# mLSTM numerators: 128-row products first, 64-row ones in pairs of row halves; mask, LN(v) and head-norm passes on ScalarE

## The chip, the cores and the metric

The kernel runs on one core of a Trainium2 chip. The metric is the device time of one execution in microseconds (us), and the median of several executions is quoted. The engines are named as the profile names them: PE is TensorE's matmuls, PEld its weight loads, DVE is VectorE, ACT is ScalarE, POOL is GpSimd and SP is the queue that issues the DMAs.

## The reference

One layer of a hybrid network works on 1024 latent tokens and 256 context tokens of width 1024. Here only the part that the change touches is written out; `h` is a normalised and modulated input.

```python
u, v, q, k, vv, o, gates = split(h @ W_in)
yA = u * (W_s @ LN(v; g_v, b_v) + b_s)      # per chunk of 128 tokens, 4 groups of 128 channels
# mLSTM, 4 heads, forward and backward, chunks of 128 tokens (rows t, sources s):
dmat    = where(tri, b_t - b_s + i_s, -inf)
w_intra = exp(dmat - m_t);   w_inter = exp(b_t + m0 - m_t)
scores  = (q k^T) * w_intra
num     = scores @ vv + w_inter * (q @ C0)  # C0: 64 x 128 state of the chunk's start
den     = sum(scores) + w_inter * (q @ n0)
h_head  = num / max(|den|, exp(-m_t))
yB      = sigmoid(o) * HeadNorm(h_fwd + h_bwd)
x = LN1(ALPHA * x + gate1 * ([yA | yB] @ W_out))
x = LN2(ALPHA * x + gate2 * SqReLU_MLP(...))
```

A head has 64 key channels and 128 value channels. So `scores @ vv` sums over 128 sources, and `q @ C0` over 64 channels.

## The kernel before

The kernel is one long program, written stage by stage in Python. A tile framework orders it: each engine works through its own list in order, the lists are laid out by the framework's scheduler, and semaphores hold an instruction until its inputs are ready and its output buffer is free. All matrix products of the projections are made of three products of rounded parts (`mm3`, lines 206 to 209: weight or activation, each split into a high and a low part); each is one pass of 512 columns. The small products of the mLSTM take float32 operands as they are, and the trace shows each of them as two passes.

The stage that the change touches (lines 802 to 830) runs from 226 to 364 us of the trace. It goes over eight chunks `j` of 128 tokens:

- `d_load(j)` loads keys `kc`, values with a column of ones `vac`, queries `qd`, and rows spread over partitions: `wib` (w_inter) and `nmb` (minus m). There is one `nmb` buffer for each direction `d`, four in all, two chunks' worth.
- `d_weights(j)` makes the weights exp(dmat - m): for each direction and head a pass on DVE (line 706) adds a column and the triangular mask, then one pass on ACT for four heads (line 707) takes the exponential. It also scales `wib` by the queries (line 708).
- `d_scores(j)` makes q k^T with 64 rows a head (line 716). Heads of even number lie on partitions 0 to 63, those of odd number on 64 to 127, and the two have PSUM banks of their own. DVE then multiplies the weights in (line 720).
- `d_out(j, d, b)` makes numerators and denominators of one direction and two heads in one PSUM bank: for each head a product of 128 rows (line 735, `vac` and the weighted scores) and one of 64 rows (line 736, the state `St` and `wib`). Direction 0 of `wib` and `St` lies on partitions 0 to 63, direction 1 on 64 to 127. Then DVE makes the reciprocal of the denominator (lines 739 to 742), and ACT (line 746) or DVE (line 748) divides.
- `d_norm(j)` normalises a head's 128 channels: statistics on DVE, a power on POOL (line 760), four passes on DVE (line 762), and a DMA to memory.

Between these stand the fillers: eight units `v_unit(j)` (24 passes of 512 columns each, then LN(v) in two DVE passes, lines 669 and 670, and later a small product `mix` with W_s, line 677, and its DVE pass, line 679) and four units `u_unit` of the same size. After each `d_out` and `d_scores` the loop takes one piece of six passes from the fillers. What is left of them runs after the loop, and then the output projection and the MLP, with 760 us to come.

[...] Banks 0 to 2 (`mm`) serve the large products, 3 and 4 (`tr`) transposes and `mix`, 5 to 7 (`nm`) the scores and numerators.

## Time and profile before

| | us |
|---|---|
| median of 3 executions | 1126.34 |
| lowest and highest | 1125.40 and 1127.55 |
| the profiled execution | 1127.33 |
| span of that execution, first to last instruction | 1125.40 |

The profile is of one execution. The span leaves out 1.93 us ahead of the first and behind the last instruction. A matmul's row in the trace is longer than its turn: passes overlap, and what counts is the distance from one start to the next. The rows are read for three things: which engine's chain ends last, how far matmuls of each kind stand apart, and what the other engines have left to do in the same stretch.

### The profile page before, as it was taken

What the parts mean: (1) busy time and instruction counts of PE and PEld (TensorE: products, weight loads), DVE (VectorE), ACT (ScalarE), POOL (GpSimd) and SP (SyncE); (2) the same over time, 40 slices, a digit from 0 to 9 for tenths busy, and PEclk for the clock granted to TensorE, in tenths of its full rate; (3) what the DMA queues carried; (4) which work ended last, traced back from release to release, by engine and by line L of the source; (5) the groups of instructions that cost most, each with busy time, mean ns of one, the idle gap of its engine ahead of it and who ended that gap; (6) DMA issues with size and microseconds to landing.
All of it is one profiled execution on the core that took longest, in us unless ns stands there. A gap on an engine that the chain in (4) does not pass through costs nothing.

```text
span 1125.4 us, 14624 instructions
## 1 busy us (share of the span) xinstructions
PE 1094.6 (97%) x5271; PEld 899.9 (80%) x5271; DVE 761.5 (68%) x1363; ACT 517.6 (46%) x821; POOL 53.6 (5%) x81
## 2 busy tenths in 40 slices
PE   8999999899999999997999999999999999999996
PEld 6899788777777888885888888888888888887875
DVE  4793666677775367659974747474667555468997
ACT  3585543321121236567755555556534334434341
POOL 0010000000101011110000000000000000001101
PEclk9999999999999999998999999999999999999999
DMA  8782579776453773233454435355997334356911
GB/s 319 259 280 95 169 255 293 236 204 175 127 155 113 260 238 129 85 112 112 151 195 127 175 123 183 112 197 201 321 413 271 113 90 152 96 168 235 326 57 75
DMA packets 92416, 208.08 MB, mean 185 GB/s; under 512 B 10037, under 2 KB 31413, under 8 KB 92089
## 3 DMA queue, kind: packets, MB, share of 16 engines
q1 hardware_dynamic: 92344, 207.16, 55.0%
q8 instruction: 41, 0.67, 0.2%
q14 instruction: 31, 0.25, 0.1%
HBM read 155.91 MB, written 51.21 MB: 184 GB/s over the span
## 4 chain that ended last, share of the span: by engine, by line
PE 89%; DVE 4%; DMA 3%; ACT 2%; issue 1%; POOL 1%; SPq 0%; DVEq 0%; ACTq 0%; POOLq 0%
PE A L986 29%; PE B L986 23%; PE wo L209 3%; PE wo L207 3%; PE wo L208 3%; PE n L736 2%; PE n L735 2%; PE pa L270 2%; PE v L207 2%; PE vg L209 1%; PE vg L208 1%; PE vg L207 1%; PE u L207 1%; PE v L209 1%; PE v L208 1%; PE u L209 1%
## 5 line engine op out<-in xcount | busy, mean ns | idle before, releaser
L986 PE MATMUL A<-wh,pb 128*128 128x512 f32 (+1 forms) x528 | 158.6, 383 | 0.0
L986 PE MATMUL B<-wh,pb 128*128 128x512 f32 x384 | 118.7, 390 | 0.0
L986 PEld LDWEIGHTS A<-wh,pb 128*128 128x128 f32 x528 | 98.0, 188 | 19.8
L986 PE MATMUL A<-wl,pb 128*128 128x512 f32 (+1 forms) x264 | 101.7, 385 | 3.2 <-DVE nmu_n L874 1.5
L986 PEld LDWEIGHTS B<-wh,pb 128*128 128x128 f32 x384 | 72.1, 188 | 15.6
L986 PE MATMUL B<-wl,pb 128*128 128x512 f32 x192 | 74.9, 390 | 0.0
L1206 ACT CAST pb<-a_S 128x1024 fp32r<-128x1024 f32 x32 | 33.7, 1053 | 75.1 <-PE B L986 43.8
L880 POOL TENSOR_TENSOR rs_n<-ve_n,mhalf 128x1 f32<-128x1 f32 x23 | 29.4, 1279 | 720.2 <-DVE ve_n L878 681.4
L1113 DVE TENSOR_TENSOR wc<-w1x,wc 128x512 fp32r<-128x512 f32 x56 | 38.3, 692 | 35.9 <-ACT wc L1112 35.9
L1207 DVE TENSOR_TENSOR wl<-b,wh 128x1024 fp32r<-128x1024 f32 x40 | 48.7, 1222 | 19.9 <-ACT wh L1206 6.9
L986 PEld LDWEIGHTS A<-wl,pb 128*128 128x128 f32 x264 | 49.6, 188 | 14.5 <-DVE nmu_n L874 1.7
L1207 DVE TENSOR_TENSOR pb<-a_S,pb 128x1024 fp32r<-128x1024 f32 x32 | 39.1, 1223 | 31.7 <-ACT pb L1206 31.5
L1206 ACT CAST wh<-b 128x1024 fp32r<-128x1024 f32 x40 | 42.0, 1051 | 33.4 <-DVE pb L1207 16.0
L207 PE MATMUL wo<-lo_W,yh 128*128 128x512 f32 x128 | 52.0, 406 | 0.0
L209 PE MATMUL wo<-hi_W,yl 128*128 128x512 f32 x128 | 50.7, 396 | 0.0
L208 PE MATMUL wo<-hi_W,yh 128*128 128x512 f32 x128 | 50.5, 394 | 0.0
L207 PE MATMUL vg<-lo_VG,Hhi 128*128 128x264 f32 x160 | 45.9, 287 | 0.0
L209 PE MATMUL vg<-hi_VG,Hlo 128*128 128x264 f32 x160 | 45.4, 284 | 0.5 <-DVE Hlo L198 0.5
L707 ACT ACTIVATE nmb<-nmb 128x512 f32<-128x512 f32 x16 | 10.1, 633 | 76.8 <-DVE nmb L706 46.6
L208 PE MATMUL vg<-hi_VG,Hhi 128*128 128x264 f32 x160 | 45.3, 284 | 0.0
L1112 ACT CAST wc<-w1x 128x512 fp32r<-128x512 f32 x56 | 34.4, 619 | 22.4 <-PE A L986 10.6
L1206 ACT CAST pb<-a_A 128x1024 fp32r<-128x1024 f32 x24 | 25.3, 1054 | 41.4 <-PE A L986 20.3
(412 smaller groups left out, 2773.7 us busy)
## 6 DMA issues: line engine op xcount, KB each, us to landing
ad<-in_wada SPq DMA_DIRECT2D x32, 512.0 KB, 6.1
b<-in_w SPq DMA_DIRECT2D x32, 512.0 KB, 5.2
a_S<-d_S SPq DMA_DIRECT2D x32, 512.0 KB, 4.1
d_S<-hF SPq DMA_DIRECT2D x50, 256.0 KB, 2.2
a_A<-d_A SPq DMA_DIRECT2D x24, 512.0 KB, 5.0
d_A<-hF SPq DMA_DIRECT2D x36, 256.0 KB, 2.0
wa<-in_wada SPq DMA_DIRECT2D x16, 512.0 KB, 6.2
w1x<-in_w SPq DMA_DIRECT2D x16, 512.0 KB, 3.6
```

What stands on the lines that cost most here:

```text
L207: T.matmul(o, ahi, blo, start=start, stop=False)
L208: T.matmul(o, ahi, bhi, start=False, stop=False)
L209: T.matmul(o, alo, bhi, start=False, stop=stop)
L270: T.matmul(pa[:, 0:256], s32[:, k, :], rv[k // 4][:, k % 4, :], start=(k == 0), stop=(k == KT - 1))
L735: T.matmul(pn[:, hh, :], nmb[d][:, h, :], vc[:, h, :], start=True, stop=False)
L736: T.matmul(pn[:, hh, :], wib[o : o + 64, h, :], st[o : o + 64, h, :], start=False, stop=True)
L880: G.tensor_tensor(rs, ve, mhalf[:, :1], op=ALU.pow)
L986: T.matmul(o, a, b, start=start and i == 0, stop=stop and i == 2, skip_group_check=more)
L1112: S.copy(t[:, 0:512], src)
L1113: V.tensor_tensor(t[:, 512:1024], src, t[:, 0:512].bitcast(F32), ALU.subtract)
L1206: S.copy(hi, src)
L1207: V.tensor_tensor(lo, src, hi.bitcast(F32), ALU.subtract)
```

## The change

It leaves the arithmetic of the layer as it is and changes its order and its engines in the stage described above.

- The numerators of both directions of two heads are made together (`d_out_mm`): four products of 128 rows, then four of 64 rows that alternate between the two halves of the partitions, in two PSUM banks. The loop puts the scores of the next chunk behind the second such group. Division stays as it was but comes as a step of its own (`d_out_ev`).
- The mask is added by one DVE pass for four heads, and the column is the bias of the exponential, which ACT now takes for each head apart: 8 passes a chunk instead of 2. The two directions share one `nmb` tile, with two buffers.
- LN(v): the second DVE pass goes; ACT scales by the reciprocal deviation. The offset `b_v` goes through W_s once, in a product `mix_bias` ahead of the loop, into the offset of the mix.
- The head norm: DVE makes a small product (`hnb`), and ACT makes the four passes.
- The numerators' ring of PSUM banks grows from three banks to five (3 to 7) for this stage, and `mix` moves to the ring of the large products.
- The loop takes two pieces of the fillers at each of three places.

```diff
--- before.py
+++ after.py
@@ -72,8 +72,10 @@
     def ps_tr(name):
         return ps_next("tr", 3, 2, name).rearrange("p (a b) -> p a b", a=4)
 
+    nm_ring = [5, 3]
+
     def ps_nm(name):
-        return ps_next("nm", 5, 3, name)
+        return ps_next("nm", *nm_ring, name)
 
 
     def prep_slot(src, n, name, colscale=None):
@@ -667,12 +669,19 @@
         mv, rs = stats(dp, pm, 512, f"v{j}")
         vc = ka.tile([P, 512], F32, tag="f2k", bufs=4, name=f"vc_{j}")
         V.scalar_tensor_tensor(vc, pm, mv[:, 0:1], lnv[:, 0, :], ALU.subtract, ALU.mult)
-        V.scalar_tensor_tensor(vc, vc, rs, lnv[:, 1, :], ALU.mult, ALU.add)
+        S.activation(vc, vc, AF.Copy, scale=rs)
         vpend.append((j, vc))
         yield
 
+    def mix_bias():
+
+        px = ps_mm("mixb").rearrange("p (a b) -> p a b", a=4)
+        for g in range(4):
+            T.matmul(px[:, g, :], lnv[:, 1, g * P : (g + 1) * P], wsT[:, g, :], start=True, stop=True)
+        V.tensor_tensor(bsb, px, bsb, ALU.add)
+
     def v_unit_mix(j, vc):
-        px = ps_tr(f"mix_{j}")
+        px = ps_mm(f"mix_{j}").rearrange("p (a b) -> p a b", a=4)
         for g in range(4):
             T.matmul(px[:, g, :], vc[:, g * P : (g + 1) * P], wsT[:, g, :], start=True, stop=True)
         mx = ka.tile([P, 4, P], F32, tag="f2k", bufs=4, name=f"mx_{j}")
@@ -686,25 +695,23 @@
         kc, vc = load_kv(j)
         qd = dp.tile([P, NH, P], F32, tag="qd", name=f"qd_{j}")
         wib = dp.tile([P, NH, P], F32, tag="wib", name=f"wib_{j}")
-        nmb = []
+        nmb = dp.tile([P, 2, NH, P], F32, tag="nmb", bufs=2, name=f"nmb_{j}")
         for d in range(2):
             o = 64 * d
             for hh in range(2):
                 dma(qd[o : o + 64, hh : hh + 3 : 2, :], d_q[64 * hh : 64 * hh + 64, :, j * P : (j + 1) * P])
             dma(wib[o : o + 64], d_rows[1, d, j].partition_broadcast(64))
-            t = dp.tile([P, NH, P], F32, tag="nmb", bufs=4, name=f"nmb_{j}_{d}")
-            dma(t, d_rows[0, d, j].partition_broadcast(P))
-            nmb.append(t)
+            dma(nmb[:, d], d_rows[0, d, j].partition_broadcast(P))
         dstate[j] = [kc, vc, qd, wib, nmb]
 
     def d_weights(j):
         kc, vc, qd, wib, nmb = dstate[j][:5]
         for d in range(2):
             r = rowbase[d](j)
-            w = nmb[d]
+            w = nmb[:, d]
+            V.tensor_tensor(w, w, mask[d].unsqueeze(1).broadcast_to([P, NH, P]), ALU.add)
             for h in range(NH):
-                V.scalar_tensor_tensor(w[:, h, :], w[:, h, :], a_cols[:, r + h : r + h + 1], mask[d], ALU.add, ALU.add)
-            S.activation(w, w, AF.Exp)
+                S.activation(w[:, h, :], w[:, h, :], AF.Exp, bias=a_cols[:, r + h : r + h + 1])
         V.scalar_tensor_tensor(wib, qd, QSCALE, wib, ALU.mult, ALU.mult)
 
     def d_scores(j):
@@ -715,37 +722,46 @@
             o = 64 * hh
             T.matmul(pss[hh][:, b * P : (b + 1) * P], kc[o : o + 64, b, :], qd[o : o + 64, h, :], start=True, stop=True)
         for hh in range(2):
+            sc = pss[hh][:, 0:256].rearrange("p (b t) -> p b t", b=2)
             for d in range(2):
-                wv = nmb[d].rearrange("p (b h) t -> p h b t", h=2)
-                V.scalar_tensor_tensor(
-                    wv[:, hh], pss[hh][:, 0:256].rearrange("p (b t) -> p b t", b=2), QSCALE, wv[:, hh], ALU.mult, ALU.mult
+                wv = nmb[:, d].rearrange("p (b h) t -> p h b t", h=2)
+                V.scalar_tensor_tensor(wv[:, hh], sc, QSCALE, wv[:, hh], ALU.mult, ALU.mult)
+
+    def d_out_mm(j, b):
+
+        kc, vc, qd, wib, nmb = dstate[j][:5]
+        pn = [ps_nm(f"n_{j}_{d}_{b}")[:, 0:258].rearrange("p (h v) -> p h v", h=2) for d in range(2)]
+        for d in range(2):
+            for hh in range(2):
+                h = 2 * b + hh
+                T.matmul(pn[d][:, hh, :], nmb[:, d, h, :], vc[:, h, :], start=hh == 0, stop=False, skip_group_check=True)
+        for hh in range(2):
+            for d in range(2):
+                h, o = 2 * b + hh, 64 * d
+                st = St[(step_f, step_b)[d](j)]
+                T.matmul(
+                    pn[d][:, hh, :], wib[o : o + 64, h, :], st[o : o + 64, h, :], start=False, stop=hh == 1, skip_group_check=True
                 )
-
-    def d_out(j, d, b):
-        kc, vc, qd, wib, nmb = dstate[j][:5]
-        if d == 0 and b == 0:
+        return pn
+
+    def d_out_ev(j, b, pn):
+        if b == 0:
             dstate[j].append(dp.tile([P, NH, P], F32, tag="hs", name=f"hs_{j}"))
         hs = dstate[j][5]
-        r = rowbase[d](j)
-        o = 64 * d
-        st = St[(step_f, step_b)[d](j)]
-        pn = ps_nm(f"n_{j}_{d}_{b}")[:, 0:258].rearrange("p (h v) -> p h v", h=2)
-        for hh in range(2):
-            h = 2 * b + hh
-            T.matmul(pn[:, hh, :], nmb[d][:, h, :], vc[:, h, :], start=True, stop=False)
-            T.matmul(pn[:, hh, :], wib[o : o + 64, h, :], st[o : o + 64, h, :], start=False, stop=True)
-        dn = dp.tile([P, 2], F32, tag="dn", bufs=4, name=f"dn_{j}_{d}_{b}")
-        den = pn[:, :, 128:129]
-        V.tensor_tensor(dn.unsqueeze(2), den, em_cols[:, r + 2 * b : r + 2 * b + 2].unsqueeze(2), ALU.max)
-        V.scalar_tensor_tensor(dn.unsqueeze(2), den, -1.0, dn.unsqueeze(2), ALU.mult, ALU.max)
-        rc = dp.tile([P, 2], F32, tag="rc", bufs=4, name=f"rc_{j}_{d}_{b}")
-        V.reciprocal(rc, dn)
-        for hh in range(2):
-            h = 2 * b + hh
-            if d == 0:
-                S.activation(hs[:, h, :], pn[:, hh, 0:P], AF.Copy, scale=rc[:, hh : hh + 1])
-            else:
-                V.scalar_tensor_tensor(hs[:, h, :], pn[:, hh, 0:P], rc[:, hh : hh + 1], hs[:, h, :], ALU.mult, ALU.add)
+        for d in range(2):
+            r = rowbase[d](j)
+            dn = dp.tile([P, 2], F32, tag="dn", bufs=4, name=f"dn_{j}_{d}_{b}")
+            den = pn[d][:, :, 128:129]
+            V.tensor_tensor(dn.unsqueeze(2), den, em_cols[:, r + 2 * b : r + 2 * b + 2].unsqueeze(2), ALU.max)
+            V.scalar_tensor_tensor(dn.unsqueeze(2), den, -1.0, dn.unsqueeze(2), ALU.mult, ALU.max)
+            rc = dp.tile([P, 2], F32, tag="rc", bufs=4, name=f"rc_{j}_{d}_{b}")
+            V.reciprocal(rc, dn)
+            for hh in range(2):
+                h = 2 * b + hh
+                if d == 0:
+                    S.activation(hs[:, h, :], pn[d][:, hh, 0:P], AF.Copy, scale=rc[:, hh : hh + 1])
+                else:
+                    V.scalar_tensor_tensor(hs[:, h, :], pn[d][:, hh, 0:P], rc[:, hh : hh + 1], hs[:, h, :], ALU.mult, ALU.add)
 
     def d_norm(j):
         hs = dstate[j][5]
@@ -758,8 +774,10 @@
         V.tensor_scalar(ve.unsqueeze(2), mv[:, :, 1:2], EPS, None, ALU.add)
         rs = dp.tile([P, NH], F32, tag="hrs", name=f"hrs_{j}")
         G.tensor_tensor(rs, ve, mhalf, op=ALU.pow)
+        nb = dp.tile([P, NH], F32, tag="hnb", name=f"hnb_{j}")
+        V.scalar_tensor_tensor(nb.unsqueeze(2), mv[:, :, 0:1], -1.0, rs.unsqueeze(2), ALU.mult, ALU.mult)
         for h in range(NH):
-            V.tensor_scalar(hs[:, h, :], hs[:, h, :], mv[:, h, 0:1], rs[:, h : h + 1], ALU.subtract, ALU.mult)
+            S.activation(hs[:, h, :], hs[:, h, :], AF.Identity, bias=nb[:, h : h + 1], scale=rs[:, h : h + 1])
         dma(d_z[j], hs.rearrange("p h v -> p (h v)"))
 
     wU = []
@@ -800,31 +818,32 @@
             yield from u_unit(ka, "f2k", 4, blk, 0)
 
     fill = fillers()
+    nm_ring[:] = [3, 5]
+    mix_bias()
     d_load(0)
     d_load(1)
     d_weights(0)
     next(fill)
     next(fill)
     d_scores(0)
-    steps = 0
     for j in range(NT):
-        todo = []
         if j + 1 < NT:
-            todo.append(lambda j=j: d_weights(j + 1))
-        todo.append(lambda j=j: d_out(j, 0, 0))
-        todo.append(lambda j=j: d_out(j, 0, 1))
+            d_weights(j + 1)
+        pn = d_out_mm(j, 0)
+        d_out_ev(j, 0, pn)
+        next(fill, None)
+        next(fill, None)
+        pn = d_out_mm(j, 1)
         if j + 1 < NT:
-            todo.append(lambda j=j: d_scores(j + 1))
-        todo.append(lambda j=j: d_out(j, 1, 0))
-        todo.append(lambda j=j: d_out(j, 1, 1))
+            d_scores(j + 1)
+        d_out_ev(j, 1, pn)
+        next(fill, None)
+        next(fill, None)
         if j + 2 < NT:
-            todo.append(lambda j=j: (d_load(j + 2), d_norm(j)))
-        else:
-            todo.append(lambda j=j: d_norm(j))
-        for i, f in enumerate(todo):
-            f()
-            if i > 0:
-                next(fill, None)
+            d_load(j + 2)
+        d_norm(j)
+        next(fill, None)
+        next(fill, None)
     run(fill)
     dd.close()
     pd.close()
```

On PE, the numerators of chunk 1 in direction 1 and around them, with the scores of chunk 2, stood before like this (`n_d_b` is the bank of direction `d` and heads 2b and 2b+1, `S_0` and `S_1` are the scores of the two halves of the partitions; one row is one float32 product, that is two passes):

```order
L677 MATMUL mix_2768<-wsT,vc_2716 128x128 x4
L716 MATMUL S_0_2776<-qd_2668,kc_2664 128x128 x2
L207 MATMUL v_2743<-lo_V_2289,Hhi 128x512
L208 MATMUL v_2743<-hi_V_2288,Hhi 128x512
L209 MATMUL v_2743<-hi_V_2288,Hlo 128x512
L207 MATMUL v_2743<-lo_V_2289,Hhi 128x512
L716 MATMUL S_1_2777<-qd_2668,kc_2664 128x128 x2
L208 MATMUL v_2743<-hi_V_2288,Hhi 128x512
L209 MATMUL v_2743<-hi_V_2288,Hlo 128x512
L207 MATMUL v_2743<-lo_V_2289,Hhi 128x512
L208 MATMUL v_2743<-hi_V_2288,Hhi 128x512
L735 MATMUL n_1_0_2792<-vac_2496,nmb_1_2508 128x129
```

and the same place reads now:

```order
L686 MATMUL mix_2773<-wsT,vc_2721 128x128 x4
L737 MATMUL n_0_1_2781<-vac_2501,nmb_2505 128x129 x2
L737 MATMUL n_1_1_2782<-vac_2501,nmb_2505 128x129 x2
L742 MATMUL n_0_1_2781<-St_1752,wib_2504 128x129
L742 MATMUL n_1_1_2782<-St_1757,wib_2504 128x129
L742 MATMUL n_0_1_2781<-St_1752,wib_2504 128x129
L742 MATMUL n_1_1_2782<-St_1757,wib_2504 128x129
L723 MATMUL S_0_2791<-qd_2666,kc_2662 128x128
L723 MATMUL S_1_2792<-qd_2666,kc_2662 128x128
L723 MATMUL S_0_2791<-qd_2666,kc_2662 128x128
L723 MATMUL S_1_2792<-qd_2666,kc_2662 128x128
L209 MATMUL v_2760<-lo_V_2289,Hhi 128x512
```

The eight products of 64 rows stand together now and alternate between the halves; before, the scores of one half stood apart from those of the other, with filler passes between. In two of the 16 groups a `mix` or filler passes come between the products of 64 rows, here for chunk 4:

```order
L737 MATMUL n_0_0_3269<-vac_3024,nmb_3028 128x129 x2
L737 MATMUL n_1_0_3270<-vac_3024,nmb_3028 128x129 x2
L742 MATMUL n_0_0_3269<-St_1755,wib_3027 128x129
L686 MATMUL mix_3250<-wsT,vc_3195 128x128 x4
L742 MATMUL n_1_0_3270<-St_1754,wib_3027 128x129
L742 MATMUL n_0_0_3269<-St_1755,wib_3027 128x129
L742 MATMUL n_1_0_3270<-St_1754,wib_3027 128x129
```

There one product of 64 rows is parted from the other three.

On DVE, the mask of chunk 4 and what surrounds it stood before like this (`hve` feeds POOL's power, `st_v`, `mv_v` and `ve_v` are the statistics of LN(v), `vc` its result):

```order
L178 BN_STATS st_v_3066<-v_2971 128x6
L756 BN_AGGR hmv_3038<-hst_3_3048 128x2
L706 SCALAR_TENSOR_TENSOR nmb_0_3031<-nmb_0_3031,cols,cst 128x128
L758 TENSOR_SCALAR hve_3051<-hmv_3038 128x4
L180 BN_AGGR mv_v_3068<-st_v_3066 128x2
L706 SCALAR_TENSOR_TENSOR nmb_0_3031<-nmb_0_3031,cols,cst 128x128
L762 TENSOR_SCALAR hs_2913<-hs_2913,hmv_3038,hrs_3053 128x128 x4
L169 TENSOR_SCALAR ve_v_3070<-mv_v_3068 128x1
L669 SCALAR_TENSOR_TENSOR vc_3074<-v_2971,mv_v_3068,lnv 128x512
L706 SCALAR_TENSOR_TENSOR nmb_0_3031<-nmb_0_3031,cols,cst 128x128
L670 SCALAR_TENSOR_TENSOR vc_3074<-vc_3074,rs_v_3072,lnv 128x512
L706 SCALAR_TENSOR_TENSOR nmb_1_3036<-nmb_1_3036,cols,cst 128x128 x4
```

and now:

```order
L712 TENSOR_TENSOR nmb_3028<-nmb_3028,cst 128x512
L772 BN_AGGR hmv_3037<-hst_3_3047 128x2
L715 SCALAR_TENSOR_TENSOR wib_3027<-qd_3026,wib_3027 128x512
L688 TENSOR_TENSOR mx_3019<-mix_3014,bsb 128x512
L774 TENSOR_SCALAR hve_3050<-hmv_3037 128x4
L712 TENSOR_TENSOR nmb_3028<-nmb_3028,cst 128x512
L778 SCALAR_TENSOR_TENSOR hnb_3054<-hmv_3037,hrs_3052 128x4
L180 BN_STATS st_v_3073<-v_3001 128x6
L182 BN_AGGR mv_v_3075<-st_v_3073 128x2
L171 TENSOR_SCALAR ve_v_3077<-mv_v_3075 128x1
L671 SCALAR_TENSOR_TENSOR vc_3081<-v_3001,mv_v_3075,lnv 128x512
```

Both mask passes stand ahead of the statistics of LN(v) now. On ACT the same chunk reads now (before, two rows of line 707 and nothing else of these):

```order
L714 ACTIVATE nmb_3028<-nmb_3028,cols 128x128 x5
L780 ACTIVATE hs_2929<-hs_2929,hnb_3054,hrs_3052 128x128 x4
L714 ACTIVATE nmb_3028<-nmb_3028,cols 128x128 x3
L672 ACTIVATE vc_3081<-vc_3081,rs_v_3079 128x512
L762 ACTIVATE hs_3105<-n_0_0_3095,rc_0_0_3109 128x128 x2
```

The scaling of `vc`, on which the next `mix` waits, stands behind the exponentials and the head norm. On every engine but SP the instructions behind this stage are the same and in the same order as before; on PE that holds from the last numerator on.

## Rows read from the trace of the kernel before

**Rows 1.** The chain that ended last, by engine, share of the span (page, part 4)

```profile
PE 89%; DVE 4%; DMA 3%; ACT 2%; issue 1%; POOL 1%; SPq 0%; DVEq 0%; ACTq 0%; POOLq 0%
```

**Rows 2.** Busy time by stretches; count, granted clock and DMA share as its header says

```profile
core 0: us, PE busy (x) PEld busy (x) DVE busy (x) ACT busy (x) POOL busy (x), PEclk, DMA share, GB/s
...
226.00:246.00 20.00, 20.00 (x102) 14.57 (x101) 16.29 (x58) 7.01 (x11) 0.55 (x1) 1.00 0.68 194
```

**Rows 3.** All that PE waited for from 226 to 390 us: total, times, longest

```profile
PE mix L677 <- DVE vc L670: 0.3, 1, 0.3
```

**Rows 4.** PE in time: start, length, engine, line, out<-in, rows*columns, count

```profile
229.33 0.39 PE L208 MATMUL v<-hi_V,Hhi 128*128 128x512 f32 x1
229.56 0.39 PE L209 MATMUL v<-hi_V,Hlo 128*128 128x512 f32 x1
229.87 0.71 PE L716 MATMUL S<-qd,kc 64*128 64x128 f32 x8
230.52 0.50 PE L207 MATMUL v<-lo_V,Hhi 128*128 128x512 f32 x1
230.86 0.39 PE L208 MATMUL v<-hi_V,Hhi 128*128 128x512 f32 x1
...
231.32 0.38 PE L735 MATMUL n<-vac,nmb 128*128 128x129 f32 x2
231.64 0.49 PE L736 MATMUL n<-St,wib 64*128 64x129 f32 x2
232.05 0.49 PE L735 MATMUL n<-vac,nmb 128*128 128x129 f32 x2
232.47 0.49 PE L736 MATMUL n<-St,wib 64*128 64x129 f32 x2
232.89 0.50 PE L207 MATMUL v<-lo_V,Hhi 128*128 128x512 f32 x1
```

**Rows 5.** PE in time: scores of one half of the partitions alone

```profile
256.21 0.71 PE L716 MATMUL S<-qd,kc 64*128 64x128 f32 x4
256.85 0.50 PE L208 MATMUL v<-hi_V,Hhi 128*128 128x512 f32 x1
```

**Rows 6.** PE in time: eight passes of 128 rows in a row

```profile
242.02 1.05 PE L677 MATMUL mix<-wsT,vc 128*128 128x128 f32 x8
242.91 0.39 PE L735 MATMUL n<-vac,nmb 128*128 128x129 f32 x2
```

**Rows 7.** Groups by line, 226 to 346 us: count, busy us and mean ns, idle before

```profile
L706 DVE SCALAR_TENSOR_TENSOR nmb<-nmb,cols,cst 128x128 f32<-128x128 f32 x64 | 19.2, 343 | 2.1 <-DMA nmb<-d_rows 2.1
L762 DVE TENSOR_SCALAR hs<-hs,hmv,hrs 128x128 f32<-128x128 f32 x24 | 6.7, 344 | 4.4 <-POOL hrs L760 4.4
L670 DVE SCALAR_TENSOR_TENSOR vc<-vc,rs_v,lnv 128x512 f32<-128x512 f32 x8 | 6.0, 746 | 0.0
L679 DVE TENSOR_TENSOR mx<-mix,bsb 128x512 f32<-128x512 f32 x8 | 5.5, 686 | 4.9 <-PE mix L677 4.9
...
L707 ACT ACTIVATE nmb<-nmb 128x512 f32<-128x512 f32 x16 | 10.1, 633 | 76.8 <-DVE nmb L706 46.6 <-issue 26.6 <-DVE hve L758 3.7
```

**Rows 8.** ACT in time: two passes of 128x128

```profile
233.65 0.63 ACT L746 ACTIVATE hs<-n,rc 128x128 f32<-128x128 f32 x2 [3.08 <-DVE rc L742]
```

**Rows 9.** SP in time, and what nmb's DMAs take from issue to landing

```profile
261.73 0.33 SPq L43 DMA_DIRECT2D vac<-d_va  x1
...
263.34 0.54 SPq L43 DMA_DIRECT2D nmb<-d_rows  x1
...
DMA to landing us min/median/max: 3.4/4.9/6.6
```

**Rows 10.** The one wait of PE, all engines in time

```profile
325.25 0.35 DVE L706 SCALAR_TENSOR_TENSOR nmb<-nmb,cols,cst 128x128 f32<-128x128 f32 x1 [0.66 <-DMA nmb<-d_rows]
...
326.32 0.38 PE L677 MATMUL mix<-wsT,vc 128*128 128x128 f32 x1 [0.33 <-DVE vc L670]
```

**Rows 11.** Weight loads of the mix products, 226 to 346 us

```profile
L677 PEld LDWEIGHTS mix<-wsT,vc 128*128 128x128 f32 x64 | 8.1, 191 | 1.4 <-DVE vc L670 0.8
```

## The prediction

> **What bounds the kernel now.** I read the chain that ended last first: PE has 89% of the span [rows 1]. [...] Then PE's waits: from 226 to 390 us, through the stage and 26 us behind it, PE waited for another engine once, for 0.3 us [rows 3]. So what ends last in this stage is PE's own list. An edit is worth what it takes off that list, and work that moves from DVE to ACT is worth nothing by itself; it matters only if it makes somebody late. Last I read the list's spacing, start to start.
>
> **What PE's passes cost.** A filler pass takes 0.23 us (229.33 to 229.56) [rows 4]. A pass of 128 rows and 128 columns takes 0.111: eight `mix` passes in 0.89 us [rows 6]. Passes of 64 rows cost a toll on both sides. The scores of chunk 0 start 0.31 us behind the last filler pass (0.08 more than it needs), their eight passes take 0.65, and the next filler pass takes 0.34 (0.11 more) [rows 4]: 0.84 for the visit. Scores of one half alone take 0.64 for four passes [rows 5], 0.83 with the same two tolls. So eight passes that alternate between the halves cost no more than four of one half: they run in pairs.
>
> What is toll and what is work follows from one `d_out`: 231.32 to 232.89 is 1.57 us, 1.68 with the 0.11 behind it [rows 4]. It holds four passes of 128 rows (0.44), four of 64 rows in one half, and two visits, since the list goes 735, 736, 735, 736. So 4 passes + 2 tolls = 1.24 and 4 passes + 1 toll = 0.83: the toll is 0.41 us a visit, a pass of 64 rows or a pair of them 0.105.
>
> **The change part by part.**
>
> Numerators. One chunk and pair of heads takes two `d_out` now, 3.36 us. Then it takes eight passes of 128 rows (0.89) and one visit of eight alternating passes (0.84, as the scores of chunk 0), 1.73 us. That is 1.63 less, 16 times: 26.1 us.
>
> Scores. Chunks 0 and 1 cost 0.84 each; the order shows chunks 2 to 7 with two visits each, 1.66 us. Sum 11.6. Then chunk 0 costs 0.84, and seven chunks follow the state products directly, so they pay four pairs (0.42 to 0.43) and no toll: 3.0. That saves 7.8 us.
>
> Taken away from that: `mix_bias` adds eight passes, 0.89 us, on PE's path. Two of the 16 groups are parted in the order, each one more toll of 0.41 and in one an unpaired product of two passes, about 0.2: 1.0 us. PE's list becomes 26.1 + 7.8 - 0.9 - 1.0 = 32.0 us shorter.
>
> DVE. The masks were 64 passes, 19.2 us, and become 16 of 512 columns, by line 679's 0.686 us [rows 7] 11.0. Line 670 goes, 6.0 us, and line 762, 32 passes of 0.344, 11.0 [rows 7]. The small product and `mix_bias`'s pass add at most eight and one passes of that 0.344 and 0.686, 3.4 together. DVE has some 21 us less in a stage that is 32 us shorter, so its share stays about where it is. ACT takes 64 exponentials for 16 of 0.633 us [rows 7]; two passes of 128 columns take 0.63 [rows 8], so 20.2 for 10.1, and 10.1 for the head norm and about 5.1 (eight of 0.633) for LN(v): 25 us more on an engine that was busy 7.01 of 20 us in its fullest window here [rows 2]. None of this lies on PE's path; PE's own list covers it, as long as results come in time.
>
> The wait that it adds. Both directions of `nmb` are one tile now, so its next load waits for all numerators of the chunk. Behind them SP issues `vac`, `wib`, `nmb`, `wib`, `nmb`; from `vac` to the first `nmb` took 1.61 us behind two `wib` [rows 9], so the second stands some 2.2 us behind the last numerator, and lands 3.4 to 6.6 us later, 4.9 in the median [rows 9]: at 7.1, with ends of 5.6 and 8.8. DVE stands at the second mask pass until then, ahead of the statistics of LN(v); ACT has the rest of the exponentials and the head norm ahead of scaling `vc`; and PE needs that `vc` for the next `mix`. This is the kind of wait that PE had once before: DVE stood 0.66 us for `nmb`, and `mix` came 0.33 us late [rows 10]. PE is there after a second's scores and exit (0.6), 12 filler passes (2.76), a `mix` (0.89), 12 passes (2.76), a group (1.73) and 12 passes (2.76): 11.5 us behind the last numerator. With the median landing the mask ends at 7.8; ACT then has one exponential, four norm passes and three exponentials at 0.31 each (2.5) and `vc` (0.63): 10.9 at the earliest, 0.6 before it is needed. With the latest landing 12.6, 1.1 late. Six loads of chunks 2 to 7 make 0 to 6.6 us. I take 2, nearer the median, since not every one is followed by a `mix` at that distance.
>
> **Sum.** 32.0 - 2.0 = 30.0 us. The profiled execution took 1127.33 us with its span of 1125.40, 1 us over the median of 1126.34. So 1097.3 against itself, and 1096.3 against the median; I say 1096.5.
>
> **A rule against it.** The `mix` passes follow each other at 0.111 us though each has a weight load of 0.191 us [rows 6, 11], so loads overlap passes of the same rows. [...] The trace contradicts it for `mix` and I give it 2 in 100.
>
> **Rivals.**
>
> The loads come later than I take them: bunched behind one wait they share the DMA engines with each other and with weights, and DVE and ACT are in order behind them. Waits of 4 to 10 us, time 1098.5 to 1104.5. For it speaks the one wait of before; against it that PE's banks and the next numerators have several us of slack.
>
> The pairs don't form for the state products: unlike the scores these add onto a bank that others have begun. Then four more pass times of 0.105 in each of 16 groups, 6.8 us: 1103. Against it: they lie as the scores lie, halves in turn and a bank for each half.
>
> The change doesn't do what it says: the order decides that, and it shows 14 of 16 groups whole. All 16 broken would cost 0.41 or 0.6 us each, 14 of which aren't in the sum: 6 to 8 us, 1104. It is in the chance of the rival before.
>
> Slower: the `nmb` loads set the pace. Then PE would have to wait more than 5.3 us at each of the six places to lose all 32. Given the 0.6 us of slack behind a median landing, the landing would have to take over 4.9 + 0.6 + 5.3 = 10.8 us from its issue; the longest was 6.6. At 12 us for each the kernel takes 1134.
>
> No change: the gain is given back behind the stage, where the output projection waits for its weights. Against it: PE waited for nothing in the 26 us behind the stage [rows 3], and the buffers for these loads come free as PE gets through the list, which moves as a whole.
>
> **How the numbers follow.** Forecast, waits up to 4 us, 1094 to 1098.5: 0.66. Late loads: 0.18. No pairs or broken ones: 0.09. The rule on weight loads: 0.02. No change: 0.03. Slower: 0.02. The range leaves out the last two and the ends of the others: 1092 (no new wait, and a little less toll than worked out) to 1104. A measurement of this kernel tells about 0.2% from no change: faster 0.95, same 0.03, slower 0.02.
>
> **What would show it.** In the profile after, a group should take about 1.7 us from its first numerator to the next filler pass, state products should start in pairs, and scores should follow them within 0.45 us. PE should still be busy all through the stage, its end some 30 us earlier, with the waits of PE listed at `mix` behind ACT's `vc`. If state products start 0.1 us apart one by one, the pairs failed. If PE's waits sum to over 10 us, DVE or ACT, or `nmb`'s landing, has become the bound, and the forecast is wrong.

## The result, and the profile after

The changed kernel takes 1107.09 us (median; 1106.29 to 1108.06) against 1126.94 before: ratio 0.983, 95% interval 0.981 to 0.984. That is 19.9 us less where 30 were forecast, and 3 us above the range.

The list of PE became what was worked out. In time order, PE in the changed kernel (as [rows 4]): a whole group of numerators, and one with the scores right behind it.

```profile
244.05 1.05 PE L737 MATMUL n<-vac,nmb 128*128 128x129 f32 x8
245.03 0.71 PE L742 MATMUL n<-St,wib 64*128 64x129 f32 x8
245.68 0.50 PE L209 MATMUL v<-lo_V,Hhi 128*128 128x512 f32 x1
246.02 0.40 PE L210 MATMUL v<-hi_V,Hhi 128*128 128x512 f32 x1
...
251.85 0.72 PE L742 MATMUL n<-St,wib 64*128 64x129 f32 x8
252.41 0.61 PE L723 MATMUL S<-qd,kc 64*128 64x128 f32 x8
252.95 0.50 PE L209 MATMUL v<-lo_V,Hhi 128*128 128x512 f32 x1
```

From 244.05 to 245.68 and the 0.11 that the next filler pass takes too long make 1.74 us; the prediction said 1.73. State products with the scores behind them end after 1.10, which is 0.45 more than the 0.65 of state products alone; it said 0.42 to 0.43.

What is new are waits. All that PE waited for from 226 to 390 us, total, times and longest (as [rows 3], which had 0.3 us):

```profile
PE mix L686 <- ACT vc L672: 6.0, 4, 3.0
PE u L209 <- DVE vc L671: 2.3, 1, 2.3
```

The windows (as [rows 2]; in each row PE's busy time is the first number behind the length, and the granted clock stands behind POOL's) show a second loss:

```profile
226.00:246.00 20.00, 20.00 (x130) 16.43 (x130) 15.89 (x51) 9.75 (x28) 0.55 (x1) 1.00 0.78 209
246.00:266.00 20.00, 17.75 (x111) 14.77 (x110) 15.27 (x59) 10.86 (x29) 3.12 (x4) 1.00 0.86 251
286.00:306.00 20.00, 17.02 (x91) 14.19 (x90) 11.02 (x42) 7.45 (x19) 1.76 (x3) 0.83 0.49 115
...
289.00:292.40 3.40, 0.43 (x3) 0.24 (x2) 2.17 (x6) 1.45 (x4) 0.55 (x1) 0.99 0.86 218
292.40:299.20 6.80, 6.79 (x23) 5.56 (x24) 2.62 (x13) 2.34 (x8) 0.00 (x0) 0.50 0.13 42
```

After the longest wait PE worked 6.8 us at a granted clock of 0.50, with filler passes 0.43 us apart (296.17 to 296.60) instead of 0.23, and by that clock lost 3.4 us. So 8.3 us of waits and 3.4 of half clock, 11.7 us, were paid out of the shorter list.

How the longest wait came about, all engines in time order (start, length; in brackets the idle time before and what ended it):

```profile
285.02 0.39 PE L211 MATMUL v<-hi_V,Hlo 128*128 128x512 f32 x1
285.44 0.70 DVE L180 BATCH_NORM_STATS2 st_v<-v 128x6 f32<-128x512 f32 x1
...
288.38 0.69 DVE L712 TENSOR_TENSOR nmb<-nmb,cst 128x512 f32<-128x512 f32 x1 [1.51 <-DMA nmb<-d_rows]
288.95 0.49 PE L742 MATMUL n<-St,wib 64*128 64x129 f32 x2
288.99 0.17 DVE L182 BATCH_NORM_AGGREGATE mv_v<-st_v 128x2 f32<-128x6 f32 x1
...
290.11 0.69 DVE L715 SCALAR_TENSOR_TENSOR wib<-qd,wib 128x512 f32<-128x512 f32 x1 [0.95 <-issue]
290.72 0.14 DVE L171 TENSOR_SCALAR ve_v<-mv_v 128x1 f32<-128x1 f32 x1
290.79 0.74 DVE L671 SCALAR_TENSOR_TENSOR vc<-v,mv_v,lnv 128x512 f32<-128x512 f32 x1
...
291.64 0.72 ACT L672 ACTIVATE vc<-vc,rs_v 128x512 f32<-128x512 f32 x1 [1.78 <-DVE vc L671]
...
292.42 2.08 PE L686 MATMUL mix<-wsT,vc 128*128 128x128 f32 x8 [2.98 <-ACT vc L672]
```

The first statistics pass of LN(v) was done at 286.1. Then DVE stood at a mask for the first `nmb` until 288.38, took the mask, the aggregate, stood at the `wib` product until 290.11, and only then made `vc`. The mask of the second `nmb` came behind that, at 291.44. The profile names no releaser for the last 0.95 us at the `wib` product; the second `wib`, issued at 283.92, landed 5.8 us later. The chain of waits of that stretch, from 280 to 296 us (start, length, what; its first row gives shares by line), names the same load:

```profile
by line: DMA wib<-d_rows 32.7%; PE mix L686 16.5%; PE n L742 11.3%; issue 9.8%; SPq L43 5.8%; PE n L737 5.6%; ACT vc L672 4.6%; PE v L209 4.5%; DVE wib L715 4.3%; DVE vc L671 4.2%; PE S L723 3.1%; DVE ve_v L171 0.4%; ACTq L672 0.2%
...
283.92 5.24 DMA wib<-d_rows
...
290.11 0.69 DVE wib L715
```

Not every wait was one for loads. For the wait of 2.3 us at `u`, DVE had stood only 0.27 us for `nmb`; two passes that round weights for a later stage (line 92) stood ahead of LN(v) there:

```profile
309.06 0.69 DVE L712 TENSOR_TENSOR nmb<-nmb,cst 128x512 f32<-128x512 f32 x1 [0.27 <-DMA nmb<-d_rows]
310.10 2.35 DVE L92 TENSOR_TENSOR lo_W<-raw_W,hi_W 128x1024 fp32r<-128x1024 f32 x2
312.37 0.69 DVE L180 BATCH_NORM_STATS2 st_v<-v 128x6 f32<-128x512 f32 x1
...
314.18 0.50 PE L209 MATMUL u<-Hlo,hi_U 128*128 128x512 f32 x1 [2.28 <-DVE vc L671]
```

For the wait of 0.8 us at 279.3, the first pass of `vc` was done at 277.51, and ACT then finished a norm pass and took three exponentials ahead of the scaling:

```profile
277.66 0.97 ACT L714 ACTIVATE nmb<-nmb,cols 128x128 f32<-128x128 f32 x3
278.54 0.71 ACT L672 ACTIVATE vc<-vc,rs_v 128x512 f32<-128x512 f32 x1
```

For each v unit I read two times from such rows, counted from the end of its last pass: when `vc` is ready, and when PE, waits aside, has come to the `mix` that needs it (for unit 7 of the changed kernel, less the 2.3 us at `u`). Unit 5 above: the last pass ends at 285.41, `vc` is ready at 292.37 (6.96), PE is free at 292.42 - 2.98 = 289.44 (4.03).

| v unit | before: vc ready | before: PE there | after: vc ready | after: PE there |
|---|---|---|---|---|
| 0 | 3.9 | 5.1 | 3.3 | 4.8 |
| 1 | 5.5 | 6.0 | 5.6 | 4.5 |
| 2 | 4.1 | 6.2 | 4.0 | 2.9 |
| 3 | 4.9 | 7.5 | 2.8 | 4.8 |
| 4 | 5.1 | 6.5 | 5.2 | 4.5 |
| 5 | 3.2 | 4.3 | 7.0 | 4.0 |
| 6 | 3.3 | 5.9 | 2.6 | 4.8 |
| 7 | 6.4 | 6.1 | 6.1 | 4.1 |
| mean | 4.55 | 5.94 | 4.57 | 4.29 |

In the mean LN(v) is no later than before. PE is 1.65 us earlier, because the groups that lie between are shorter, and `vc` comes unevenly: 2.6 to 4.0 us where no mask stands ahead, up to 7.0 where DVE waits for loads.

### The profile page after: what moved, and what is told of

It is laid out like the page before. It is cut to its first block, busy times and chain, and to the rows that moved or that the text cites. A ratio compares the mean times of both kernels' runs of the same rounds, so it can differ in the third digit from the quotient of the medians.

```text
span 1103.4 us, 14609 instructions
## 1 busy us (share of the span) xinstructions
PE 1065.2 (97%) x5279; PEld 885.6 (80%) x5279; DVE 743.2 (67%) x1284; ACT 543.9 (49%) x909; POOL 52.8 (5%) x81
## 4 chain that ended last, share of the span: by engine, by line
PE 85%; DVE 5%; DMA 4%; ACT 2%; issue 1%; POOL 1%; SPq 0%; DVEq 0%; ACTq 0%; POOLq 0%
PE A L1005 29%; PE B L1005 23%; PE wo L211 3%; PE wo L209 3%; PE wo L210 3%; PE pa L272 2%; DMA nmb<-d_rows 2%; PE vg L211 2%; PE vg L210 1%; PE vg L209 1%; PE u L209 1%; PE u L210 1%; PE u L211 1%; PE o L211 1%; PE o L209 1%
## 5 line engine op out<-in xcount | busy, mean ns | idle before, releaser
L1226 DVE TENSOR_TENSOR wl<-b,wh 128x1024 fp32r<-128x1024 f32 x40 | 48.7, 1221 | 19.9 <-ACT wh L1225 6.9
L1226 DVE TENSOR_TENSOR pb<-a_A,pb 128x1024 fp32r<-128x1024 f32 x24 | 29.3, 1221 | 21.1 <-ACT pb L1225 21.0
```

The source lines that it names most:

```text
L1226: V.tensor_tensor(lo, src, hi.bitcast(F32), ALU.subtract)
```

## The experiments

All kernels have the changed one as their base, but for one that starts from the kernel before; diffs show what differs. An edit also lets the framework set the order on DVE, ACT and SP anew where times change in its own estimate, so a difference of 2 or 3 us can come from that (e8 gained its 3.3 us that way). PE's order stays nearly the same; the largest difference is e14's, where the scores stand in 11 pieces (8 or 9 in the others with the new order). In the table, waits are PE's from 226 to 390 us; half clock is (1 - granted clock) x 20 us summed over the windows from 226 to 366; the rest is the span less both.

| kernel | median us | ratio to before, 95% | span | waits | half clock | rest |
|---|---|---|---|---|---|---|
| changed | 1107.1 | 0.981-0.984 | 1103.4 | 8.3 | 3.4 | 1091.7 |
| e1 products alone | 1102.2 | 0.977-0.981 | 1100.3 | 4.7 | 1.8 | 1093.8 |
| e2 third nmb | 1101.7 | 0.975-0.981 | 1100.8 | 5.9 | 5.2 | 1089.7 |
| e3 vc on DVE | 1110.8 | 0.985-0.989 | 1109.0 | 11.3 | 7.2 | 1090.5 |
| e4 norm on DVE | 1102.3 | 0.978-0.981 | 1100.7 | 6.6 | 1.8 | 1092.3 |
| e5 mix 0-6 later | 1105.1 | 0.980-0.983 | 1104.0 | 8.7 | 5.2 | 1090.1 |
| e6 other bank | 1105.9 | 0.981-0.984 | 1103.1 | 8.5 | 5.2 | 1089.4 |
| e7 all mix later | 1102.0 | 0.978-0.981 | 1100.5 | 5.3 | 3.4 | 1091.8 |
| e8 moves alone | 1122.1 | 0.996-0.998 | 1118.4 | 0.0 | 0.0 | 1118.4 |
| e9 masks behind LN | 1097.6 | 0.972-0.976 | 1096.0 | 3.8 | 0.0 | 1092.2 |
| e10 and third nmb | 1095.1 | 0.970-0.974 | 1093.9 | 2.6 | 0.0 | 1091.3 |
| e11 and mix later | 1093.1 | 0.969-0.972 | 1092.4 | 0.9 | 0.0 | 1091.5 |
| e12 two nmb tiles | 1100.1 | 0.975-0.979 | 1097.6 | 5.2 | 1.8 | 1090.6 |
| e13 e11 in sequence | 1092.5 | 0.968-0.972 | 1089.7 | 1.1 | 0.0 | 1088.6 |
| e14 e9 without moves | 1101.7 | 0.977-0.980 | 1099.1 | 3.9 | 3.4 | 1091.8 |

The last column is the main finding: in the 14 kernels with the new order of products it is 1091.1 in the mean and within 2.7 of it in each. Before it is 1125.4 - 0.3 = 1125.1, which is 34 us more. The column is what is left of one execution's whole span, so it carries what varies outside of the stage too. Inside the stage, from the first V pass to the first pass behind the last U pass, the kernel before and then the changed one show:

```profile
226.93 0.50 PE L207 MATMUL v<-lo_V,Hhi 128*128 128x512 f32 x1
388.98 0.60 PE L864 MATMUL pzt<-cst,zt 128*128 128x128 f32 x4
```

```profile
227.10 0.47 PE L209 MATMUL v<-lo_V,Hhi 128*128 128x512 f32 x1
367.83 0.60 PE L883 MATMUL pzt<-cst,zt 128*128 128x128 f32 x4
```

That is 162.05 and 140.73 us; without waits and half clock 161.7 and 129.0, so 32.7 less, and 31.8 once the 0.9 of `mix_bias`, which stands ahead of the first V pass, is counted. The same reading of the other kernels with the new order gives 30.1 to 33.2 (32.0 were worked out). So the list became shorter about as forecast in all of them, and they differ mainly by what PE waits and by the half clock behind the waits.

**First: loads, moves to ACT, or DVE's load?** The new order of products with DVE's old work (masks, LN(v), head norm):

```
-            V.tensor_tensor(w, w, mask[d]..., ALU.add)          # and exponentials by head with bias
+            V.scalar_tensor_tensor(w[:, h, :], ..., mask[d], ALU.add, ALU.add)   # as before, for four heads
-        S.activation(vc, vc, AF.Copy, scale=rs)
+        V.scalar_tensor_tensor(vc, vc, rs, lnv[:, 1, :], ALU.mult, ALU.add)
-            S.activation(hs[:, h, :], hs[:, h, :], AF.Identity, bias=nb..., scale=rs...)
+            V.tensor_scalar(hs[:, h, :], hs[:, h, :], mv..., rs..., ALU.subtract, ALU.mult)
-    mix_bias()
```

> The changed kernel with only the new order of the products: masks, second pass of LN(v) and head norm are on DVE in their old form, and there is no mix_bias. The list of PE is then 32.9 us shorter than before (32.0 and the 0.9 of mix_bias). Theory 'loads' (the waits of the changed kernel, 9 us, and the half clock, 3.5 us, come from nmb and wib landing late, with DVE in order behind them): the waits stay, 1104 to 1109. Rival 'ACT' (they come from the passes that were moved to ACT ahead of vc): they vanish, 1093 to 1097. Rival 'DVE' (a list of PE that is 30 us shorter needs DVE's 21 us to be gone, since DVE was busy 102 of 140 us): slower than the changed kernel, 1109 to 1120, with waits of PE for DVE in many places.

1102.2: none of the three. It is 4.9 us faster than the changed kernel, so there the moves to ACT cost time on balance. The waits moved; the largest is at the scores, for a bank that ACT empties:

```profile
PE S L723 <- ACT hs L762: 2.4, 3, 1.7
PE u L209 <- DVE vc L671: 1.6, 1, 1.6
PE mix L686 <- DVE vc L672: 0.7, 1, 0.7
```

A third buffer for `nmb` (the shift row of `lnv`, which is read once, borrows one of them for room), with the loads in a function of their own:

```
-        nmb = dp.tile([P, 2, NH, P], F32, tag="nmb", bufs=2, ...)
+        nmbs[j] = dp.tile([P, 2, NH, P], F32, tag="nmb", bufs=3, ...)
         pn = d_out_mm(j, 0)
+        if j + 2 < NT:
+            n_load(j + 2)
```

> The changed kernel with a third buffer for nmb, and its two loads for chunk j+2 issued behind the first numerators of chunk j, about one chunk (some 14 us) earlier; the loads of vac, wib and qd stay where they are. Theory 'loads': DVE no longer stands for nmb, PE's waits at mix and u fall from 9 us to under 4 (what wib causes stays), the clock does not fall, 1096 to 1101. Rival 'ACT': DVE's waits for nmb go, but PE's waits stay, 1104 to 1108.

1101.7, just above the range of 'loads', and not as told: PE's waits fell to 5.9 only, and the clock fell twice. DVE's waits for `nmb` halved (6.1 to 3.2 us) and those at the `wib` product fell too (5.5 to 2.1); those for POOL in the same stretch rose (4.3 to 6.2).

Second LN pass, and head norm, each back on DVE:

```
-        S.activation(vc, vc, AF.Copy, scale=rs)
+        V.tensor_scalar(vc, vc, rs, None, ALU.mult)
```

> The changed kernel with the scaling of vc back on DVE (8 passes), mix_bias kept. Rival 'ACT': vc no longer stands behind exponentials and head norm, PE's waits go, 1094 to 1098. Theory 'loads': only the share of ACT goes (at three of the five waits ACT stood 0.7 to 1.5 us between vc's first pass and its scaling), the longest wait stays, 1102 to 1107.

```
-            S.activation(hs[:, h, :], hs[:, h, :], AF.Identity, bias=nb..., scale=rs...)
+            V.tensor_scalar(hs[:, h, :], hs[:, h, :], mv..., rs..., ALU.subtract, ALU.mult)
```

> The changed kernel with the 32 head norm passes back on DVE. Rival 'ACT': four passes fewer ahead of vc on ACT, about 1.2 us at each wait, 1099 to 1103. Theory 'loads': DVE gets 11 us more in front of LN(v), and the waits for loads stay, 1106 to 1112.

1110.8 is slower than either theory said; 1102.3 is what 'ACT' said. The two moves pull in opposite ways, so 'ACT' as a whole is not the cause; both edits also changed DVE's order, and neither isolates ACT's part.

**Second: PE's distance.** From the table of v units I expected that a later `mix` would be enough.

```
-            if kt == 3 and vpend:
+            if kt == 7 and vpend:
                 v_unit_mix(*vpend.pop())
```

> The changed kernel with one thing changed in the source: the mix of chunk j stands behind the last K slice of the next v unit instead of the fourth. In PE's order mix 0 to 6 come 12 to 28 passes later behind the last pass of their v unit; mix 7 stays. Theory 'deadline': LN(v) takes as long as before (from the last v pass to the ready vc 2.6 to 7.0 us in the changed kernel, mean 4.57; before 3.2 to 6.4, mean 4.56), but PE, whose list is shorter, is at mix after 4.5 us in the mean instead of 5.9. With the mix some 2.8 us later the four waits at mix (6.0 us) and the half clock behind the longest (3.5) are gone: 1096.5 to 1099. Theory 'loads' in its first form: DVE's delay by nmb and wib reaches PE at another place (numerators, scores, u), and 1103 to 1107 stays.

1105.1, in the range of 'loads': my theory 'deadline' fell, and with it its premise on LN(v), for in this kernel `vc` is ready after 6.6 us in the mean, at most 10.4. PE is at `mix` after 7.5 to 16.8 us now, and only one of the waits there is left, but it waits at the scores instead, 4.6 us, since the evictions of the numerators stand behind DVE's waits for loads (8.7 us at the masks). The wait at `u` I tried by itself, with another PSUM bank:

```
-        px = ps_mm(f"mix_{j}")...
+        px = (ps_nm if j == NT - 1 else ps_mm)(f"mix_{j}")...
```

> The changed kernel with the PSUM tile of mix 7 alone in the ring of the numerators' banks, so that the first u unit gets a bank that is already free, and not the one of v 7, for whose first LN pass it waited 2.3 us. Reason 'bank' (the move of mix into the ring of v and u made this wait): 2.3 us go, 1104.5 to 1105.2. Reason 'late LN': v 7's vc was ready 6.1 us behind its last pass; PE, without the wait at u, is at mix 7 after 4.1 us and waits 2 us there instead: 1106.5 to 1107.5.

1105.9, between the two answers in time; the waits decide. The one at `u` is gone, and `mix` 7 waits 3.0 us. So the bank was not what mattered: LN(v) of unit 7 was late, behind two rounding passes of line 92 as in the changed kernel. With all eight `mix` later:

```
             yield from u_unit(ka, "f2k", 4, blk, 0)
+            if blk == 0:
+                v_unit_mix(*vpend.pop())      # and kt == 7 as above
```

> As the run with mix 0 to 6 later, and mix 7 stands behind the first u unit besides, which so takes an older bank. Theory 'deadline': no wait of PE over 0.3 us is left from 226 to 346 us, clock 1.00 throughout, 32.0 us less than before as worked out: 1094 to 1096. If 'loads' or 'ACT' hold, PE waits at other instructions: 1100 to 1106.

1102.0, in the range of 'loads or ACT': PE waits 4.1 us at the scores for ACT's `hs` again, up to 2.7 at once.

The moves to ACT alone, on the kernel before:

> The kernel before with only the moves from DVE to ACT: mask pass of 512 columns with exponentials by head, second pass of LN(v) and head norm on ACT, and mix_bias. The order of the products, two tiles for nmb and the banks are as before. Theory 'deadline': PE's distances are those of before, no wait of more than 1 us, and mix_bias costs 0.9: 1126 to 1129. Rival 'ACT': vc stands behind exponentials and head norm as in the changed kernel, PE waits 3 to 6 us at mix: 1130 to 1135.

1122.1: 3.3 us faster, and PE waits for nothing. With the moves LN(v) is ready after 3.7 us in the mean there (4.55 before). So the moves don't make `vc` late by themselves. The gain is in PE's list: in this order the scores stand in 10 pieces instead of 15 (chunk 4's had three, where the prediction counted two). In both kernels each piece stands between fillers or `mix`, so that is five tolls (0.41) less, and in four chunks the halves pair, four times four passes (0.42) less: 3.7 us, and 0.89 more for `mix_bias`: 2.8, inside of what the interval of the ratio leaves (2.0 to 4.4).

**Third: DVE's order.** Loads, buffers and ACT's work as in the changed kernel; only the masks and the `wib` product of the next chunk stand behind the first LN pass of the last finished v unit, by an edge that sets order and no wait:

```
-        lnp: first LN pass of v_unit, kept
-            d_weights(j + 1)
+            with tc.issue_after(lnp[0]) if lnp else ExitStack():
+                d_weights(j + 1)
```

> The changed kernel with an order on DVE alone: the mask passes and the wib product of the next chunk stand behind the first LN pass of the last v unit that is complete in the program (in the changed kernel they stood ahead of it at five of the eight units). The loads, their buffers and ACT's work are as in the changed kernel. Theory 'order' (DVE stands at the masks for nmb and wib with LN(v) behind it): vc is ready 2.6 to 4.2 us behind the last v pass, as in the units of the changed kernel where no mask stood ahead (2.6 to 4.0), PE's four waits at mix and the half clock go, 1095 to 1099, with up to 2.3 us left at u. Rival 'loads limit by themselves': the delay passes to the numerators' side, PE waits at n or S for ACT or DVE: 1102 to 1106.

1097.6, as 'order' said, 9.5 us faster than the changed kernel, with no half clock. DVE's waits at the masks for `nmb` are as long as in the changed kernel (6.1 us); LN(v) doesn't stand behind them any more. `vc` is ready after 3.96 us in the mean. PE's waits, and then the window in which the changed kernel had the half clock (columns as above):

```profile
PE mix L687 <- ACT vc L673: 1.4, 2, 0.8
PE S L724 <- ACT hs L763: 1.3, 1, 1.3
PE u L209 <- DVE vc L672: 1.1, 1, 1.1
```

```profile
286.00:306.00 20.00, 18.51 (x126) 15.60 (x124) 14.68 (x51) 12.20 (x26) 2.41 (x5) 1.00 0.74 188
```

With the third `nmb` and `mix` 7 behind the first `u` unit, and then with the other `mix` later too:

> As the run with the masks behind LN(v), with the third buffer for nmb and its loads a chunk earlier, and with mix 7 behind the first u unit. Theory 'order' with the loads out of the way: PE waits less than 1 us from 226 to 346 us and the whole list of 32.0 us is there: 1094 to 1096.5. If the run without these two has the same time, the loads cost nothing once LN(v) stands ahead. If PE still waits over 3 us, something besides masks and loads is late: 1099 to 1103.

> As the run with order, third nmb and mix 7 behind the first u unit, and mix 0 to 6 behind the last K slice of the next v unit besides, which gives LN(v) 2.8 us more. Theory 'order': nothing is left to gain, within 1 us of the run without it, 1094 to 1096.5. Rival 'deadline alone' (what counts is PE's distance, not what stands ahead of LN): it is faster than that run by 3 us or more.

1095.1, in the range of 'order', though PE waits 2.6 us where less than 1 was expected; and 1093.1, 14 us under the changed kernel and 34 under the one before. In e11 PE waits 0.9 us in all:

```profile
PE S L730 <- ACT hs L769: 0.9, 2, 0.6
```

The later `mix` gives 2.0 us here, more than expected and less than the 3 of 'deadline alone', and as much as in e5. But here PE's waits fall with it (2.6 to 0.9 us); in e5 they did not (8.3 to 8.7).

**Fourth: parts of the sum.** The single tile, on which the prediction laid the late loads:

```
-        nmb = dp.tile([P, 2, NH, P], F32, tag="nmb", bufs=2, ...)
+        nmb = [dp.tile([P, NH, P], F32, tag="nmb", bufs=4, ...) for d in range(2)]
```

> The changed kernel with a tile of its own for each direction of nmb again (four buffers, as before the change). The prediction laid the late loads on the single tile. If that is so, the first direction's load can start earlier, DVE's waits at the masks and PE's at mix shrink: 1099 to 1104. If not (in the new order of the products both directions are read to the end in the same group of 1.6 us, so that neither tile is free before the other by more than 0.3 us): 1106 to 1108, with the waits of the changed kernel.

1100.1: the tile matters, but not where I had said. DVE's waits at the masks did not shrink (6.1 to 6.8 us); those at the `wib` product did (5.5 to 2.6), and PE's longest wait went from 3.0 to 1.7. Of the 7 us, waits and half clock make 4.7. SP's queue for the same chunk shows how, in the changed kernel and then with two tiles:

```profile
282.04 0.55 SPq L43 DMA_DIRECT2D vac<-d_va  x1
282.70 0.48 SPq L43 DMA_DIRECT2D wib<-d_rows  x1
283.53 0.33 SPq L43 DMA_DIRECT2D nmb<-d_rows  x1
283.92 0.49 SPq L43 DMA_DIRECT2D wib<-d_rows  x1
284.47 0.57 SPq L43 DMA_DIRECT2D nmb<-d_rows  x1
```

```profile
278.72 0.33 SPq L43 DMA_DIRECT2D nmb<-d_rows  x1
279.15 0.57 SPq L43 DMA_DIRECT2D d_mix<-mx  x1
280.15 0.32 SPq L43 DMA_DIRECT2D vac<-d_va  x1
280.57 1.16 SPq L43 DMA_DIRECT2D wib<-d_rows  x2
281.79 0.58 SPq L43 DMA_DIRECT2D nmb<-d_rows  x1
```

The first `nmb` goes 1.4 us ahead of `vac` instead of 1.5 behind it. The state products in sequence by half, in e11:

```
-        for hh in range(2):
-            for d in range(2):
+        for d in range(2):
+            for hh in range(2):
```

> The run with order, third nmb and later mix, with the state products of a group in sequence by row half (two of the lower 64 rows, then two of the upper) instead of in turn; PE's order is otherwise the same. Theory 'pairs': two products of different halves run at the same time, and in sequence only the middle two do; one to two more pass times of 0.105 us and up to a toll in each of 16 groups, 1.7 to 6.7 us more: 1095 to 1100. If the products run one by one in either order: no change, 1092.5 to 1094.

1092.5, no change, but not for the reason given: one by one, eight passes of 0.105 would take 0.84 us. They take 0.65, in sequence as in turn:

```profile
242.33 0.72 PE L749 MATMUL n<-St,wib 64*128 64x129 f32 x8
242.98 0.50 PE L209 MATMUL v<-lo_V,Hhi 128*128 128x512 f32 x1
```

And the moves undone where DVE's order is right:

> The new order of the products with the masks and the wib product behind LN(v), and without the moves to ACT (masks, second pass of LN(v) and head norm on DVE in their old form, no mix_bias). To be set beside the run with the order and the moves (1097.6) and the one with the products alone (1102.2). If DVE bears its old work once LN(v) stands ahead: 1095 to 1098.5, the moves to ACT are worth nothing. If DVE, with about 20 us more in a stage that is 32 us shorter, is the bound: 1100 to 1106, the moves are worth 3 to 8 us.

1101.7 against 1097.6: with the order of e9 the moves to ACT are worth 4.1 us. DVE is busy 18.58 us of 20 in a window of e14 (16.18 in e9). That DVE's load as such is the bound is not shown: PE waits as long in both (3.9 and 3.8 us), and what differs is a half clock of 3.4 us behind one wait of 2.3 at the scores, and the scores in 11 pieces instead of 8. Against e1 (1102.2) the order alone gives nothing that can be told from no change; it pays only together with the moves.

## Why the prediction missed

- **PE's list: right.** Toll, pair and group as in the first fence; 31.8 us by the stage, 32.0 worked out. The table's 34 holds some 2 us from outside of the stage.
- **Weight loads: nothing for them in the longer runs, as the sum had it.** Eight 128-row passes start 0.98 us before the state products in the first fence, 0.111 each and an entry, though each of their weight loads takes 0.192 us (median; 0.186 to 0.193). No run here shows a term for weight loads, to which the prediction gave 0.02; in its place the runs of eight kept the distance that `mix` had.
- **Work on ACT: right in size but for the head norm.** Groups by line of the changed kernel from 226 to 346 us (as [rows 7]): exponentials 20.8 us (20.2 said), scalings of `vc` 5.7 (5.1), head norm 0.48 a pass where 0.31 was taken.

```profile
L714 ACT ACTIVATE nmb<-nmb,cols 128x128 f32<-128x128 f32 x64 | 20.8, 390 | 20.1 <-DVE nmb L712 11.8 <-DVE hmv L772 7.7 <-DVE mv_v L182 0.6
L780 ACT ACTIVATE hs<-hs,hnb,hrs 128x128 f32<-128x128 f32 x28 | 11.6, 482 | 13.3 <-DVE hnb L778 13.3
...
L672 ACT ACTIVATE vc<-vc,rs_v 128x512 f32<-128x512 f32 x8 | 5.7, 718 | 10.9 <-DVE dn L755 8.0 <-DVE vc L671 1.8 <-POOL rs_v L173 0.8
```

- **"Worth nothing by itself": wrong.** Alone the moves gave 3.3 us, through the order of the scores (e8). Under the new order of products they cost 4.9 as DVE's order stood in the changed kernel (e1), and gave 4.1 once masks stood behind LN(v) (e9 against e14).
- **The wait that it adds: the step that failed.** It took 2.0 us of a range of 0 to 6.6; waits measured 8.3. The mechanism named (loads behind all numerators, DVE's masks ahead of LN(v)) holds for a part: e9 shows that the order on DVE matters, e12 that the single tile does. Loads stood in front of LN(v) at three of the five waits (1.2, 0.8 and 3.0 us), at the second of them with ACT's passes behind. The 2.3 at `u` came behind two weight passes, which the prediction did not look at. The 1.1 at 260.0 had no mask in front: `vc` took 4.0 us, and PE was there after 2.9. Three things in the working on loads were off. The second `nmb` landed 7.9, 8.7 and 9.1 us behind the issue of `vac` at three chunks (7.1 taken, 5.6 to 8.8 as ends). `wib` was left out, though DVE stood for it: at the longest wait the first `nmb` and `wib` held LN(v), one behind the other, and the second `nmb`, on which the working rests, did not. And PE was counted at `mix` 11.5 us behind the last numerator; before the longest wait it was there after 7.5 (281.9 to 289.4), since 24 filler passes and a part of a group lay between, not 36, a group and a `mix`. The distance should have been read from each v unit's end to its `mix`, and shortened by what the change takes out between them.
- **The half clock: not in the sum.** The prediction put nothing for it; it took 3.4 us. It was gone, with a granted clock of 1.00 in every window, where no pause was longer than 1.5 us (e9, e10, e11, e13).
- **Rivals.** 'The loads come later' had waits of 4 to 10 us and came nearest; its price of 1098.5 to 1104.5 lacked the clock, and 3.4 of the 8.3 us (at `u` and at 260.0) had another cause. That the loads are slow because they share the DMA engines, as it says, no run tried. 'No pairs' was wrong, and e13 shows that the turn, which I gave as the reason against it, is not needed.

The sum with measured terms: 31.8 less list, 8.0 more waits (8.3 against 0.3) and 3.4 of half clock leave 20.4 us; the medians differ by 19.9. The two spans differ by 22.0, since the profiled executions also differ by 1.6 us outside of the stage, where the kernels do the same.

What stays open: why, in e2 and e7, a delay at the masks shows at one instruction of PE and not at another, was read from the traces and not tried. Nor was a kernel tried in which the weight passes stand behind LN(v) of unit 7.

## What to carry to other kernels

When an edit shortens the list of the engine that sets the pace, every result that was just in time becomes late by the same amount: read, for each thing that this engine will wait for, how long it takes and how far away its use is, and subtract what the edit removes in between. An instruction that waits for a load must not stand ahead of one on which the pace depends, on an engine that takes its list in order as DVE did here (LN(v)'s aggregate could start at 286.1 and started at 288.99); setting that order alone gave 9.5 us here, nearly half of what the change itself had given (and nothing with the moves undone, so such an edge is to be tried and not counted on). And price a new pause with a slow clock that may follow it, not by its length alone: here 3.4 us behind a pause of 2.98.

## What the runs showed of the hardware

- A pause of TensorE cost as much again as its length in the changed kernel: behind 2.98 us of waiting the granted clock was 0.50 for 6.8 us, which is 3.4 us lost. By the windows of all these kernels the granted clock stayed at 1.00 behind each pause of up to 1.5 us, and was lower behind twelve of the fourteen of 2.2 us and more (0.83 to 0.91 in the window of the pause), but not behind the 2.28 at `u` in the changed kernel or the 2.9 there in e4; of the four between (1.6 to 1.8 us) it was lower behind three (0.91). What decides between them no run here shows.
- Products on the two halves of the rows ran side by side: in the changed kernel eight passes start in four pairs 6 to 7 ns apart, from 245.03 to 245.48, and take 0.65 us, where four passes of one half alone took 0.64 [rows 5]. The eight took 0.65 us also where both products of one half stood ahead of both of the other in PE's list (e13, 242.33 to 242.98). The rows don't say which half each is, and the order of the list is taken from the source.
- VectorE and ScalarE did their work in order in the rows shown here: in the rows of the longest wait, LN(v)'s aggregate, whose input was there at 286.1, starts at 288.99 behind the mask, and the step after it at 290.72 behind the `wib` product. On ScalarE the scaling of `vc`, whose input was there at 277.51, starts at 278.54 behind three exponentials.
